# A hybrid decoder step on one core: two merges of a triangular inverse on column strips, adaLN gates by 512 columns, and 73 unread products at the start

## The chip, the cores and the metric

The kernel runs on one core of a Trainium2 chip. The metric is the device time of one execution in microseconds (us). Before the change three runs gave 2180.27, 2182.63 and 2183.85 us; the median is 2182.63 us. TensorE is called PE in the profile, its weight loads PEld, VectorE DVE, ScalarE ACT, GpSimd POOL and SyncE SP.

## The reference

One layer of a decoder trunk, for 1024 new positions of one sequence and one token each of eight others. What is computed, cut to what the change touches:

```python
mod = silu(c) @ w_ada + b_ada                   # (2048) @ (2048, 6144), 1 + 8 conditioning vectors
shift, scale, gate = split(mod, 3)
h = rmsnorm(x, norm_g) * (1 + scale) + shift
z = h @ w_in                                    # (1024 + 8, 2048) @ (2048, 8208)
...                                             # group A: gated short convolutions on half of z
# group B, per head and chunk: the gated delta rule in WY form
lmat = (k * beta) @ k.T * decay_strict
tmat = inverse(eye + lmat)                      # lower triangular
...                                             # u, o and the state by tmat, chunk after chunk
y = concatenate([y_a, o]) @ w_out               # (1024 + 8, 2048) @ (2048, 2048)
out = rmsnorm(x + gate * y, final_norm_g)
```

Everything is float32. There are 8 heads of 128 channels; the kernel takes chunks of 128 positions, four per head and half of the sequence.

## The kernel before, in words

**Layout.** Activations stand transposed: channels on the 128 partitions, positions along the free axis. The sequence is taken in two halves of 512 positions; the eight single tokens ride along with the second. The large products (`w_in`, `w_out`) split both operands into a high and a low part (`whi`/`wlo` by `split_w`, `hh`/`hl` by `make_h`, `yhi`/`ylo`) and add three products of the parts, `hh*whi`, `hl*whi` and `hh*wlo`. These are the rows `mm<-hh,whi` and so on, 512 columns wide in the first half, 256 and 264 in the second; they are most of the program.

**Stages.** First, per 128 channels, shift and scale come from `w_ada` (tiles `wat`), the normalised input `h` is made, and the first seven products with `w_in` are run beside that. Then the products of half 0 run, head by head and group by group in the hand-written table of `order`, with the delta-rule chains of the heads threaded between them. The output product of half 0 follows, then the same for half 1.

**What sets the order of the work.** The instruction order on all engines is fixed when the program is built. The class `_Order` keeps a planned time for each engine: each recorded product advances it by its `cost`, generators (`od.spawn`) wait for a planned time or for tiles (`yield`), and `pump` steps those that are due between two large products. So a changed `cost` or another number of instructions in one generator moves the positions of all later steps on every engine.

**The inverse.** For each head and half, `gdn_invert` solves the 32x32 diagonal blocks on DVE (rows `ob`, `xb`), with a round trip through memory. `gdn_apply` joins them into the 128x128 inverse `Y` of each of the four chunks. Two small merges join pairs of 32x32 blocks (`cht<-xc,dU`, then `cht<-yc,pt` and `cht<-pt,yc`). Two merges then join the halves: `pp` is the 64x64 product of `dU[0:64, c, 64:128]` and `X` (rows `cht<-X,dU`, lines 962 to 965 of the kernel), ACT writes it to `pb`, and `py` is the 64x64 product of `pb` and `Y` (rows `cht<-Y,pb`), which ACT writes to `Y`. In the order's and the trace's rows the moving operand stands behind the arrow first and the stationary one after it, as in `cht<-X,dU`. The four chunks use the same place in the array, rows 0 to 63 and columns 64 to 127 for the first of these merges, rows 64 to 127 and columns 0 to 63 for the second. After them come, per chunk, the products `cht<-st,kq`, `cht<-rt,Y`, `cht<-u,kt` and `ot<-u,dA`.

**The gates.** `gate_chunks` makes the third part of `mod` (tile `ga`, used in the output products as the factor of `y`). It runs between the large products of half 0, started 60 us of planned time after them by `conditions`, and is followed by `x1_stats`, which reads the second half of `x`. For each 128 gate columns `f`, 16 tiles of `sc` (silu of the conditioning, 32 columns of which 9 are used) are the stationary operand and blocks of `w_ada` of 128x128 the moving one; block `k` goes to column strip `k % 4` of the array, so that each strip holds a quarter of the sum. They are loaded by SP as `gw` tiles, four blocks of 128x128 to a tile, in rows of 128 numbers, and used 8 products at a time with a planned pause (`GATES`) of 7 us. After four `f` the bank is copied to `evg`, and four products with the 10-column table `selada` add the strips and transpose; four `tensor_scalar` add the bias. The tiles `gw` and `evg` share a ring of five buffers (`fx`). `raw`, the tiles of `w_in` and `w_out`, are loaded on the same SP queue, with four buffers and four more for the split parts.

**The beginning.** `norm` adds the squares of the first half of `x` on ACT, DVE and, for four of the sixteen tiles, PE (`cht<-sqt,cs`); until then PE has nothing to do. `ones` is a tile of ones that POOL writes.

PE instructions appear in the order's listing once; a float32 product counts as two records of the trace, and a transpose of one block as one.

Of the kernel before, what the change touches and what calls it, by code (L numbers as in the profile page):

```python
# [11 lines left out]
ALU = mybir.AluOpType  # L12
AX = mybir.AxisListType
# [3 lines left out]
P = 128  # L17
D = 2048
# [366 lines left out]
def _trunk(ctx, tc, nc, xT, w_in, w_ada, w_out, pack, consts, vecs, csq, ssm, yT, cap, cqp, ssp, cas, cqs, sss):  # L385
# [24 lines left out]
    def ch_tile():  # L410
        return ps_g.tile([P, 512], F32, tag="ch", name="cht", bufs=2)
# [17 lines left out]
    def pkv(n, a=0, w=None):  # L429
        o, ww = PK[n]  # L430
        return pk[:, o + a:o + a + (ww if w is None else w)]

    def ck(n, a=0, w=None):
        o, ww = CK[n]
        return cs[:, o + a:o + a + (ww if w is None else w)]
# [483 lines left out]
    def gdn_apply(half, h, hd, gp, done, cx, kq, yt):  # L919
# [41 lines left out]

        pp = ch_tile()
        for c in range(NC):
            mm(pp[64:128, c * 64:c * 64 + 64], dU[0:64, c, 64:128], X[0:64, c, 0:64], cost=0.06, start=True, stop=True,
               tile_position=(0, 64))
        pb = gp.tile([P, NC, 64], F32, tag="pb", name="pb", bufs=1)
        S.activation(pb[64:128], pp[64:128, :NC * 64].rearrange("p (c s) -> p c s", c=NC), AF.Copy, scale=-1.0)
        yield SOON
        py = ch_tile()
        for c in range(NC):  # L970
            mm(py[0:64, c * 64:c * 64 + 64], pb[64:128, c, :], Y[64:128, c, 64:128], cost=0.112, start=True, stop=True,
               tile_position=(64, 0))
        S.activation(Y[0:64, :, 64:128], py[0:64, :NC * 64].rearrange("p (c s) -> p c s", c=NC), AF.Copy)
        yield

# [402 lines left out]
            ws.add(w_out, m * P, ROWS)  # L1378


    def fx_tile(name):
        return tp.tile([P, WH], F32, tag="fx", name=name, bufs=FX)

# [19 lines left out]
    with ExitStack() as pools:  # L1403
# [38 lines left out]
        def fill(t, most=1000):  # L1442

            while most and od.now < t and queue and od.ready(hs[queue[0][0]][1], False) <= od.now:
                if next(queue[0][1], True):
                    queue.pop(0)
                most -= 1

        for _ in range(4):
            load_ada()  # L1450
        ws.ahead(0)
# [75 lines left out]
        yield  # L1527
        yield from rstd_of(acc, WH, rstd)

    GATES = 7.0  # L1530

    def gate_chunks():

        tiles = []

        def load(i):
            f, kq = divmod(i, 4)
            wt = fx_tile("gw")
            src = w_ada[kq * 512:(kq + 1) * 512, 2 * D + f * P:2 * D + (f + 1) * P]
            SY.dma_start(wt[:, :512].rearrange("p (k n) -> p k n", n=P), src.rearrange("(k p) n -> p k n", p=P))  # L1540
            tiles.append(wt)
        for i in range(4):
            load(i)
        for f in range(NK):
            if f % 4 == 0:
                ps = mm_tile()
                od.pin(ps)
            for i in (4 * f, 4 * f + 2):
                yield GATES
                yield [tiles[i][:], tiles[i + 1][:], LAND]  # L1550
                for k in range(i % 4 * 4, i % 4 * 4 + 8):
                    j = k % 4
                    mm(ps[32 * j:32 * j + 32, f % 4 * P:(f % 4 + 1) * P], sc[:, k, :],
                       tiles[f * 4 + k // 4][:, j * P:(j + 1) * P], cost=0.096 if k % 8 else 0.18,
                       start=(k < 4), stop=(k >= 12), tile_position=(0, 32 * j))
                tiles[i] = tiles[i + 1] = None
                for j in (4, 5):
                    if i + j < 4 * NK:
                        load(i + j)
            if f % 4 < 3:  # L1560
                continue
            ev = fx_tile("evg")
            S.activation(ev[:, :512], ps[:], AF.Copy)
            od.pinned.discard(ps[:].tensor.name)
            yield [ev[:, :512]]
            p2 = ch_tile()
            for i in range(4):
                mm(p2[:, i * 10:i * 10 + 10], ev[:, i * P:(i + 1) * P], ck("selada"), start=True, stop=True)
            for i in range(4):
                V.tensor_scalar(ga[:, f - 3 + i, :], p2[:, i * 10:i * 10 + 9], pkv("bada", 29 + f + i, 1), None, ALU.add)  # L1570

    conditioned = []

# [290 lines left out]
```

## Time and profile before

| what | value |
|---|---|
| median of three runs | 2182.63 us |
| the profiled execution's own time | 2179.28 us |
| its span, first to last instruction | 2177.5 us |
| PE busy, of the span | 2116.6 us (97%) |
| DVE, ACT, POOL busy | 1243.7, 829.3, 826.4 us |
| mean granted clock of PE | 0.99 |
| DMA traffic | 299.65 MB, 138 GB/s on average |

The profiled execution is 3.35 us below the median, and 1.78 us of its time lie outside the span. Times in rows of the trace are counted from the first instruction. In a row of the timeline the first number is the start, the second the length of the merged instructions, and the brackets hold the time for which the engine stood idle before it and what it waited for. Products are pipelined: the length of a row holds the drain, which overlaps with the next row, so what a product takes from the engine is the distance from its start to the start of the next. For the large products of half 0 that distance is about 0.23 us.

### The profile page before, as it was taken

The numbers are of one execution on the slowest core, as the hardware profiler recorded it, in microseconds if no ns is written. First come the engines' busy times: TensorE is split into PE (matmuls) and PEld (weight loads), VectorE is DVE, ScalarE is ACT, GpSimd is POOL, SyncE is SP. The second block draws the span as 40 slices with busy tenths as digits, with TensorE's granted clock in tenths as the row PEclk, the third lists the DMA queues.
The fourth block names the chain that finished last, engine by engine and source line by source line (L and its number), as shares of the span: only waits on it lengthen the run. The fifth ranks groups of instructions, "written<-read, shape, count | busy, mean of one in ns | idle before, by whom it ended". The sixth has DMA issues, their size and how long they took to land. (4 is left out here: it accounts for less than half of the span.)

```text
span 2177.5 us, 40451 instructions
## 1 busy us (share of the span) xinstructions
PE 2116.6 (97%) x15045; PEld 1858.7 (85%) x15045; DVE 1243.7 (57%) x3653; ACT 829.3 (38%) x1887; POOL 826.4 (38%) x801
## 2 busy tenths in 40 slices
PE   6999999999999999999999999999999999999996
PEld 3568777777778888878889999999999999999996
DVE  3436766745967636278124747657486486345544
ACT  3224333333443432353233334343343433344553
POOL 1223333433433434332434333344433343444453
PEclk8999999999999999999999999999999999999999
DMA  9984766887544456865434565557673445878777
GB/s 298 327 237 82 157 141 152 136 134 128 135 110 92 90 99 86 76 176 177 148 108 110 122 122 106 118 101 107 105 96 82 96 100 96 90 91 231 213 215 214
DMA packets 507557, 299.65 MB, mean 138 GB/s; under 512 B 37600, under 2 KB 486880, under 8 KB 507360
## 3 DMA queue, kind: packets, MB, share of 16 engines
q1 hardware_dynamic: 484656, 285.31, 61.9%
q10 hardware_dynamic: 22704, 11.77, 2.2%
q8 instruction: 118, 1.93, 0.4%
q14 instruction: 79, 0.65, 0.1%
HBM read 277.06 MB, written 19.94 MB: 136 GB/s over the span
## 5 line engine op out<-in xcount | busy, mean ns | idle before, releaser
L323 POOL TENSOR_TENSOR wlo<-raw,whi 128x512 fp32r<-128x512 f32 x529 | 709.1, 1343 | 1242.3 <-ACT whi L323 1067.9
L372 PE MATMUL mm<-hh,whi 128*128 128x264 f32 (+1 forms) x3008 | 972.5, 323 | 6.3 <-DVE y L323 2.1
L372 PE MATMUL mm<-hl,whi 128*128 128x264 f32 (+1 forms) x3008 | 971.0, 323 | 1.9 <-DVE hl L323 1.9
L372 PE MATMUL mm<-hh,wlo 128*128 128x264 f32 (+1 forms) x3008 | 971.3, 323 | 0.3 <-POOL wlo L323 0.3
L323 ACT ACTIVATE whi<-raw 128x512 fp32r<-128x512 f32 x672 | 418.8, 628 | 622.7 <-PE mm L372 377.6
L372 PEld LDWEIGHTS mm<-hh,whi 128*128 128x128 f32 x3008 | 568.5, 189 | 54.4 <-issue 8.5
L372 PEld LDWEIGHTS mm<-hl,whi 128*128 128x128 f32 x3008 | 568.8, 189 | 43.5 <-DVE hl L323 3.6
L372 PEld LDWEIGHTS mm<-hh,wlo 128*128 128x128 f32 x3008 | 568.6, 189 | 40.4 <-issue 1.0
L372 PE MATMUL mm<-yhi,wlo 128*128 128x512 f32 (+2 forms) x768 | 248.0, 323 | 6.7 <-DVE wlo L323 4.8
L372 PE MATMUL mm<-yhi,whi 128*128 128x512 f32 (+2 forms) x768 | 246.4, 321 | 0.3 <-ACT whi L323 0.2
L372 PE MATMUL mm<-ylo,whi 128*128 128x512 f32 (+2 forms) x768 | 246.2, 321 | 0.0
L323 DVE TENSOR_TENSOR ob<-tb,xb 128x62 f32<-128x62 f32 (+30 forms) x992 | 195.7, 237 | 3.9 <-DMA tb<-ub 3.9
L323 DVE TENSOR_TENSOR xb<-xb,ob 128x62 f32<-128x62 f32 (+30 forms) x992 | 193.6, 235 | 0.0
L323 DVE TENSOR_TENSOR wlo<-raw,whi 128x512 fp32r<-128x512 f32 x143 | 107.1, 754 | 98.5 <-ACT whi L323 76.4
L372 PEld LDWEIGHTS mm<-yhi,wlo 128*128 128x128 f32 x768 | 144.5, 188 | 21.7 <-DVE wlo L323 6.9
L372 PEld LDWEIGHTS mm<-ylo,whi 128*128 128x128 f32 x768 | 144.7, 188 | 12.6 <-issue 1.0
L372 PEld LDWEIGHTS mm<-yhi,whi 128*128 128x128 f32 x768 | 144.6, 188 | 12.1 <-ACT whi L323 0.9
L323 DVE SCALAR_TENSOR_TENSOR kq<-zr,pk,kq 128x512 f32<-128x512 f32 x96 | 103.5, 1078 | 3.4
L323 DVE SCALAR_TENSOR_TENSOR res<-mm,ga,xr 128x512 f32<-128x512 f32 (+2 forms) x48 | 27.3, 569 | 110.7 <-PE mm L372 101.1
L323 DVE TENSOR_TENSOR acc<-acc,sqt 128x512 f32<-128x512 f32 (+3 forms) x71 | 54.7, 773 | 26.1 <-ACT sqt L323 25.1
L323 DVE SCALAR_TENSOR_TENSOR rt<-cht,gt_neg,v 128x128 f32<-128x128 f32 x56 | 19.5, 348 | 72.0 <-PE cht L372 72.0
L323 ACT ACTIVATE u<-cht,sm 128x128 f32<-128x128 f32 x64 | 23.5, 367 | 89.1 <-DVE u L323 76.0
(403 smaller groups left out, 1979.8 us busy)
## 6 DMA issues: line engine op xcount, KB each, us to landing
raw<-in_w_in SPq DMA_DIRECT2D x488, 256.0 KB, 5.0
raw<-in_w_out SPq DMA_DIRECT2D x160, 256.0 KB, 3.4
wat<-in_w_ada SPq DMA_DIRECT2D x64, 512.0 KB, 7.3
gw<-in_w_ada SPq DMA_DIRECT2D x64, 256.0 KB, 6.2
tb<-ub ACTq DMA_DIRECT2D x16, 512.0 KB, 6.5
raw<-in_w_in SPq DMA_DIRECT2D x48, 128.0 KB, 6.0
sl<-in_ssm SPq DMA_DIRECT2D x12, 512.0 KB, 6.3
x1s<-in_xT SPq DMA_DIRECT2D x16, 260.0 KB, 5.2
```

The costliest lines, as they stand in the source:

```text
L323: r = f(*args, **kw)
L372: r = self.pe.matmul(out, lhsT, rhs, **kw)
```

## The change

Three edits, and what they move.

In the two merges each 64x64 product is cut into two of 64 rows by 32 columns on two neighbouring column strips; four products become eight, and the planned cost becomes 0.06 us for each of the eight in both merges (before 0.06 for each of four in the first and 0.112 in the second).

The gates are made 512 columns at a time: a `gw` tile is 128 rows of `w_ada` by 512 columns, four of them are loaded at a time and used by four products of 512 columns, one on each strip. 256 products of 128 columns become 64 of 512, in 16 groups with a planned pause of 14 us in place of 32 with 7. Four transposes take the place of the four products with `selada`, a `tensor_reduce` over the strips and a `tensor_tensor` with the bias that of the four `tensor_scalar`.

At the beginning, `busy(73)` writes 73 products of a 32x32 corner of `ones` with itself to a bank that nobody reads.

```diff
         pp = ch_tile()
         for c in range(NC):
-            mm(pp[64:128, c * 64:c * 64 + 64], dU[0:64, c, 64:128], X[0:64, c, 0:64], cost=0.06, start=True, stop=True,
-               tile_position=(0, 64))
+            for q in (64, 96):
+                mm(pp[q:q + 32, c * 64:c * 64 + 64], dU[0:64, c, q:q + 32], X[0:64, c, 0:64], cost=0.06,
+                   start=True, stop=True, tile_position=(0, q))
...
         py = ch_tile()
         for c in range(NC):
-            mm(py[0:64, c * 64:c * 64 + 64], pb[64:128, c, :], Y[64:128, c, 64:128], cost=0.112, start=True, stop=True,
-               tile_position=(64, 0))
+            for q in (0, 32):
+                mm(py[q:q + 32, c * 64:c * 64 + 64], pb[64:128, c, q:q + 32], Y[64:128, c, 64:128], cost=0.06,
+                   start=True, stop=True, tile_position=(64, q))
...
+    def busy(n):
+        t = ch_tile()
+        for _ in range(n):
+            mm(t[:32, :32], ones[:32, :32], ones[:32, :32], cost=0.047, start=True, stop=True)
...
+        busy(73)
         for _ in range(4):
             load_ada()
...
-    GATES = 7.0
+    GATES = 14.0
...
-        def load(i):
-            f, kq = divmod(i, 4)
-            wt = fx_tile("gw")
-            src = w_ada[kq * 512:(kq + 1) * 512, 2 * D + f * P:2 * D + (f + 1) * P]
-            SY.dma_start(wt[:, :512].rearrange("p (k n) -> p k n", n=P), src.rearrange("(k p) n -> p k n", p=P))
...
+                k, f = i % NK * P, 2 * D + i // NK * 512
+                SY.dma_start(tiles[i][:, :512], w_ada[k:k + P, f:f + 512])
...
-                for k in range(i % 4 * 4, i % 4 * 4 + 8):
-                    j = k % 4
-                    mm(ps[32 * j:32 * j + 32, f % 4 * P:(f % 4 + 1) * P], sc[:, k, :],
-                       tiles[f * 4 + k // 4][:, j * P:(j + 1) * P], cost=0.096 if k % 8 else 0.18,
-                       start=(k < 4), stop=(k >= 12), tile_position=(0, 32 * j))
...
+            for j in range(4):
+                mm(ps[32 * j:32 * j + 32, :], sc[:, k + j, :], tiles[i + j][:, :512], cost=0.23 if j else 0.41,
+                   start=(k == 0), stop=(k == 12), tile_position=(0, 32 * j))
+                tiles[i + j] = None
+            for _ in range(4):
+                load()
...
-            for i in range(4):
-                mm(p2[:, i * 10:i * 10 + 10], ev[:, i * P:(i + 1) * P], ck("selada"), start=True, stop=True)
-            for i in range(4):
-                V.tensor_scalar(ga[:, f - 3 + i, :], p2[:, i * 10:i * 10 + 9], pkv("bada", 29 + f + i, 1), None, ALU.add)
+            for j in range(4):
+                mm(p2[:, j * P:(j + 1) * P], ev[:, j * P:(j + 1) * P], ident, is_transpose=True)
+            f = i // NK * 4
+            V.tensor_reduce(ga[:, f:f + 4, :], mk(p2[:], 0, [[P, 4], [1, 9], [32, 4]]), AX.X, ALU.add)
+            V.tensor_tensor(ga[:, f:f + 4, :], ga[:, f:f + 4, :],
+                            pkv("bada", 32 + f, 4).unsqueeze(2).to_broadcast([P, 4, 9]), ALU.add)
```

What PE has in its queue at the first head's merges of half 0, before the change: a group of the gates (two `gw` tiles of four products each), and one product later the first of the two merges.

```order
L372 MATMUL mm_2693<-hh_326,wlo_2561 128x512
L372 MATMUL mm_2028<-gw_2520,sc_128 32x128 x4
L372 MATMUL mm_2028<-gw_2522,sc_128 32x128 x4
L372 MATMUL mm_2693<-hh_326,whi_2560 128x512
L372 MATMUL cht_2721<-X_2640,dU_1842 64x64 x4
L372 MATMUL mm_2693<-hl_327,whi_2560 128x512
```

The same place on PE after the change, at the second of the two merges.

```order
L372 MATMUL mm_2731<-hh_400,whi_2610 128x512
L372 MATMUL cht_2764<-Y_2676,pb_2751 32x64 x8
L372 MATMUL mm_2731<-hl_401,whi_2610 128x512
L372 MATMUL mm_2102<-gw_2597,sc_128 32x512
L372 MATMUL mm_2102<-gw_2599,sc_128 32x512
L372 MATMUL mm_2102<-gw_2601,sc_128 32x512
L372 MATMUL mm_2102<-gw_2603,sc_128 32x512
L372 MATMUL mm_2731<-hh_400,wlo_2611 128x512
```

A merge has become eight products in a row, a gate group four products of 512 columns from four tiles; the groups stand about 65 rows of the queue apart in place of about 33, and so fall at other places among the chains.

The SP queue in the gates' stage, before: two gate tiles between every two or three tiles of `w_in`.

```order
L323 DMA raw_2366<-in_w_in 128x4x128
L323 DMA raw_2402<-in_w_in 128x4x128
L323 DMA gw_2440<-in_w_ada 128x4x128
L323 DMA gw_2442<-in_w_ada 128x4x128
L323 DMA raw_2460<-in_w_in 128x4x128
L323 DMA raw_2482<-in_w_in 128x4x128
L323 DMA raw_2502<-in_w_in 128x4x128
L323 DMA gw_2520<-in_w_ada 128x4x128
L323 DMA gw_2522<-in_w_ada 128x4x128
```

And after.

```order
L323 DMA raw_2226<-in_w_in 128x4x128
L323 DMA gw_2236<-in_w_ada 128x512
L323 DMA gw_2238<-in_w_ada 128x512
L323 DMA gw_2240<-in_w_ada 128x512
L323 DMA gw_2242<-in_w_ada 128x512
L323 DMA raw_2281<-in_w_in 128x4x128
L323 DMA raw_2314<-in_w_in 128x4x128
L323 DMA raw_2356<-in_w_in 128x4x128
L323 DMA raw_2386<-in_w_in 128x4x128
L323 DMA raw_2416<-in_w_in 128x4x128
L323 DMA gw_2440<-in_w_ada 128x512
```

Four gate tiles now stand together, with four to six tiles of `w_in` between the fours. On PE the 73 products stand first in the queue, ahead of `cht<-sqt,cs`; up to the first gate group the rest of PE's queue is unchanged.

More of the change, by code (lines that the diff above doesn't have):

```diff
@@ L1528, in x1_stats, with load @@
         yield from rstd_of(acc, WH, rstd)
-    GATES = 7.0
+    GATES = 14.0
     def gate_chunks():
         tiles = []
-        def load(i):
-            f, kq = divmod(i, 4)
-            wt = fx_tile("gw")
-            src = w_ada[kq * 512:(kq + 1) * 512, 2 * D + f * P:2 * D + (f + 1) * P]
-            SY.dma_start(wt[:, :512].rearrange("p (k n) -> p k n", n=P), src.rearrange("(k p) n -> p k n", p=P))
-            tiles.append(wt)
-        for i in range(4):
-            load(i)
-        for f in range(NK):
-            if f % 4 == 0:
+        def load():
+            i = len(tiles)
+            if i < 4 * NK:
+                tiles.append(fx_tile("gw"))
+                k, f = i % NK * P, 2 * D + i // NK * 512
+                SY.dma_start(tiles[i][:, :512], w_ada[k:k + P, f:f + 512])
+        for _ in range(4):
+            load()
+        for i in range(0, 4 * NK, 4):
+            k = i % NK
+            if k == 0:
                 ps = mm_tile()
                 od.pin(ps)
-            for i in (4 * f, 4 * f + 2):
-                yield GATES
-                yield [tiles[i][:], tiles[i + 1][:], LAND]
-                for k in range(i % 4 * 4, i % 4 * 4 + 8):
-                    j = k % 4
-                    mm(ps[32 * j:32 * j + 32, f % 4 * P:(f % 4 + 1) * P], sc[:, k, :],
-                       tiles[f * 4 + k // 4][:, j * P:(j + 1) * P], cost=0.096 if k % 8 else 0.18,
-                       start=(k < 4), stop=(k >= 12), tile_position=(0, 32 * j))
[L1556 to L1560, printed above, removed]
+            yield GATES
+            yield [t[:] for t in tiles[i:i + 4]] + [LAND]
+            for j in range(4):
+                mm(ps[32 * j:32 * j + 32, :], sc[:, k + j, :], tiles[i + j][:, :512], cost=0.23 if j else 0.41,
+                   start=(k == 0), stop=(k == 12), tile_position=(0, 32 * j))
+                tiles[i + j] = None
+            for _ in range(4):
+                load()
+            if k < 12:
                 continue
@@ L1565, in gate_chunks @@
             yield [ev[:, :512]]
+            while held["ch"]:
+                yield 0.2
             p2 = ch_tile()
-            for i in range(4):
-                mm(p2[:, i * 10:i * 10 + 10], ev[:, i * P:(i + 1) * P], ck("selada"), start=True, stop=True)
-            for i in range(4):
-                V.tensor_scalar(ga[:, f - 3 + i, :], p2[:, i * 10:i * 10 + 9], pkv("bada", 29 + f + i, 1), None, ALU.add)
+            for j in range(4):
[4 more added lines that the diff above has]
+                            pkv("bada", 32 + f, 4).unsqueeze(2).to_broadcast([P, 4, 9]), ALU.add)
     conditioned = []
```

## The prediction

> **What bounds the kernel.** I read the page first, then the busy time by stretches, then the waits of PE. The page's line of busy times:
>
> ```profile
> PE 2116.6 (97%) x15045; PEld 1858.7 (85%) x15045; DVE 1243.7 (57%) x3653; ACT 829.3 (38%) x1887; POOL 826.4 (38%) x801
> ```
>
> PE is the only engine near its span. That is an average, so the stretches come next: the beginning, and all that follows it (PE, PEld, DVE, ACT, POOL busy, then the granted clock, the DMA share and GB/s).
>
> ```profile
> 18.50:35.50 17.00, 11.96 (x103) 8.92 (x104) 6.46 (x9) 3.76 (x7) 5.23 (x4) 0.50 1.08 265
> 56.00:59.40 3.40, 2.91 (x28) 1.33 (x32) 2.81 (x6) 3.08 (x5) 1.19 (x1) 0.51 1.10 348
> 59.40:2177.00 2117.60, 2079.59 (x14757) 1837.69 (x14749) 1222.40 (x3615) 808.90 (x1853) 818.93 (x788) 0.99 0.64 133
> ```
>
> From 59.4 us on PE is busy for 2079.6 of 2117.6 us: 38.0 us are left for all waits together. So a microsecond taken from PE's queue there comes off the end, unless it turns into a wait. Before that, the DMA share is 1.08 and 1.10 and the clock is at half for 17 us: another regime. The waits of PE from 60 us on show what could take a gain back: many kinds, each of a few us, the longest single one 2.1 us.
>
> ```profile
> PE mm L372 <- DVE wlo L323: 4.8, 6, 1.6
> PE cht L372 <- DVE acc L323: 3.7, 2, 2.1
> ...
> PE cht L372 <- ACT pb L323: 1.6, 1, 1.6
> ```
>
> The sum is therefore made of what each group of small products takes from PE, start to start.
>
> **The gates.** A group of the gates in the timeline of PE, between large products:
>
> ```profile
> 310.10 0.40 PE L372 MATMUL mm<-hl,whi 128*128 128x512 f32 x1
> 310.43 0.64 PE L372 MATMUL mm<-gw,sc 128*32 128x128 f32 x16
> 311.00 0.50 PE L372 MATMUL mm<-hh,wlo 128*128 128x512 f32 x1
> 311.34 0.40 PE L372 MATMUL mm<-hh,whi 128*128 128x512 f32 x1
> ```
>
> From 310.10 to 311.34 are 1.24 us, of which two large products would take 2 x 0.23; the group costs 0.78 us. It is 0.57 of its own (310.43 to 311.00) and about 0.21 for going over to strips and back. There are 512 records in all, 16 to a group, so 32 groups, 25.0 us:
>
> ```profile
> L372 PE MATMUL mm<-gw,sc 128*32 128x128 f32 x512 | 20.7, 279 | 0.0
> ```
>
> No product of 512 columns on four strips is in this trace, but the first stage has the same shape at 256 columns, in groups of four and of eight products (8 and 16 records):
>
> ```profile
> 88.52 1.07 PE L372 MATMUL tpt<-wat,sc 128*32 128x256 f32 x16
> 89.52 0.50 PE L372 MATMUL cht<-hh,whi 128*128 128x512 f32 x1
> ...
> 90.42 0.64 PE L372 MATMUL tpt<-wat,sc 128*32 128x256 f32 x8
> 90.99 0.50 PE L372 MATMUL ot<-hh,whi 128*128 128x512 f32 x1
> ```
>
> The four of 256 columns take 0.57 us, exactly as the eight of 128: it is columns that cost, not instructions. The eight of 256 take 1.00, so 1024 more columns cost 0.43 and 0.14 is fixed. Four products of 512 columns have the columns of the latter: 1.00, with the same 0.21 around them 1.21 us. Sixteen groups are 19.4 us in place of 25.0: **5.6 us less**. The saving is that of sixteen fixed parts of 0.35 us. If a 512-column stream ran no better than separate groups (1.56 for two), it would be nothing; if the fixed part vanished altogether (16 x 0.86 = 13.8) it would be 11.2. I take 5.6, since the rows at 256 columns are the same instruction at half the length.
>
> The four `selada` products against a group of four transposes of 128x128 blocks:
>
> ```profile
> 521.66 0.95 PE L372 MATMUL cht<-cs,evg 128*128 128x10 f32 x8
> 522.47 0.48 PE L372 MATMUL mm<-hl,whi 128*128 128x512 f32 x1
> ```
>
> ```profile
> 212.99 0.60 PE L372 MATMUL tpt<-cs,v 128*128 128x128 f32 x4
> 213.34 0.48 PE L372 MATMUL mm<-hh,wlo 128*128 128x512 f32 x1
> ```
>
> 0.81 becomes 0.35, four times: **1.8 us less**. What DVE does with them (one reduction and one addition over 36 columns in place of four small operations) lies beside PE; the bank they read has a second one behind it, and `ga` is read only by the output products. I cost it at nothing. If PE waited for it each time, the whole of a 512-column operation on DVE is an upper bound, 0.75 us four times, 3.0 us:
>
> ```profile
> L323 DVE TENSOR_TENSOR wlo<-raw,whi 128x512 fp32r<-128x512 f32 x143 | 107.1, 754 | 98.5 <-ACT whi L323 76.4
> ```
>
> The loads: SP issues the same 64 transfers of 256 KB, four in a row in place of two, and the tiles of `w_in` stand behind them. PE has the split parts of several tiles in hand, so this is cover as long as these are there. Where it is thinnest, from 400 to 520 us, the transfers take (KB each, us to landing):
>
> ```profile
> raw<-in_w_in SPq DMA_DIRECT2D x34, 256.0 KB, 7.1
> gw<-in_w_ada SPq DMA_DIRECT2D x24, 256.0 KB, 7.6
> ```
>
> I cost it at nothing and keep the other case as a rival.
>
> **The merges.** One of them, and the nearest group of products on two places of the array at once:
>
> ```profile
> 291.72 0.68 PE L372 MATMUL cht<-X,dU 64*64 64x64 f32 x8
> 292.32 0.50 PE L372 MATMUL mm<-hl,whi 128*128 128x512 f32 x1
> ```
>
> ```profile
> 287.25 0.44 PE L372 MATMUL cht<-xc,dU 32*32 32x32 f32 x16
> 287.62 0.50 PE L372 MATMUL mm<-hh,wlo 128*128 128x512 f32 x1
> ```
>
> A merge takes 0.60 us: 0.14 fixed, as above, and 0.46 for eight records one after another, 0.058 each. After the change there are eight records on each of two strips, each still 64 columns. In the `wat` rows the eight further records are two of 256 columns on each of four strips and cost 0.43, that is 0.84 ns per column of a strip, so eight of 64 take 0.43, and with the fixed part 0.57 if the strips run side by side. That is 0.03 less. Both kinds have 128 records in all, eight to a merge, so 32 merges:
>
> ```profile
> L372 PE MATMUL cht<-Y,pb 64*64 64x64 f32 x128 | 10.8, 224 | 1.6 <-ACT pb L323 1.6
> L372 PE MATMUL cht<-X,dU 64*64 64x64 f32 x128 | 10.8, 225 | 0.0
> ```
>
> **1.0 us less.** Cutting a product by its stationary columns does not shorten the stream that each strip must see. The bounds: the `xc` group, 16 records in 0.37, would give 7.4 us less, but its stream is 32 columns and the merges' is 64; strips that take turns would need 16 x 0.058 + 0.14 = 1.06 a merge, 14.7 us more. I take 0.57, which follows the rows with strips.
>
> The rows that speak for side by side are the gates': 16 records of 128 columns in 0.57 us on strips that share all 128 rows, whose weight loads lie inside that time:
>
> ```profile
> 240.89 0.45 PEld L372 LDWEIGHTS mm<-gw,sc 128*32 128x32 f32 x16 [0.36 <-issue]
> ```
>
> The Trainium skill, page "TensorE: Matmul & The Clock Gate", Part 3, says that a weight load overlaps with products in flight only where its row group differs; the two strips of a merge share their rows, so by that rule they would take turns and the sum would be 7.3 us worse than no change in place of 8.4 better. The trace disagrees for the gates' strips, and no merge on strips is in it.
>
> **The 73 products.** Until its first product PE only waits, and what the 73 need, `ones`, POOL has written by 0.93 us; below it stand PE's first row and two later waits that end with a transfer:
>
> ```profile
> 0.73 0.20 POOL L323 MEMSET ones<- 128x128 f32 x1 [0.29 <-POOLq L1841]
> ```
>
> ```profile
> 8.47 3.71 PE L372 MATMUL cht<-sqt,cs 128*128 128x512 f32 x4 [8.47 <-ACT sqt L323]
> ...
> 51.54 0.64 PE L372 MATMUL tpt<-wat,sc 128*32 128x256 f32 x8 [0.92 <-DMA wat<-in_w_ada]
> 53.05 0.64 PE L372 MATMUL tpt<-wat,sc 128*32 128x256 f32 x8 [0.87 <-DMA wat<-in_w_ada]
> ```
>
> The `xc` group has eight products on two places, 0.23 us beyond the fixed part, so 0.058 for one product on one place; 73 take 4.2 us at full clock and 8.4 at half, and end between 5 and 9.4 us. At worst the first `sqt` product starts 0.9 us late, with a faster clock to make it up. What could be won is PE time before 53 us, and there PE stands waiting for `wat` to land: any lead ends in a longer wait. The half clock from 18.5 to 35.5 us begins 9 us or more after the last of the 73. So **nothing**; bounds 2 us either way. The same page, Part 1, has the clock fall back after an idle window of about 3.4 us; the trace agrees in kind, with 0.50 in the row from 18.50.
>
> **Sum.** 5.6 + 1.8 + 1.0 = 8.4 us. The profiled execution of 2179.28 would take 2170.9; it lies 3.35 below the median, so the median of 2182.63 becomes **2174.2 us**. About 0.2%, 4.4 us, is what a measurement of this kernel can tell from no change: faster is below 2178.3, slower above 2187.0.
>
> **Rivals.** *New waits eat it.* The order is re-planned, and almost every row behind the first gate group stands elsewhere among the chains. A misplaced step costs up to 2.1 us of wait, and a pause can bring a half-clock window after it, as at 56 us (3.4 us at 0.51: 1.7 lost). Two such, 2 x 3.8 = 7.6, give 2181.8, no change. For: the waits of 38.0 us are of just this kind. Against: as many can vanish as appear. Chance 0.20.
>
> *More than the sum.* The gates' tiles come in rows of 512 numbers in place of 128, the crowded stretch eases, and the wait for `pb` (1.6, with 1.7 of half clock behind it) goes; if also 1.8 of the half clock in the beginning reached the end: 8.4 + 3.3 + 1.8 = 13.5, 2169.1 us. Against: the wait for `pb` is one among many. Chance 0.15.
>
> *The strips of a merge take turns.* 14.7 more in the merges against 7.4 less in the gates: 2189.9 us, slower. It decides once a merge takes 0.23 us more than before (0.83 in place of 0.60). Against: the gates' strips. Chance 0.07.
>
> *Four loads in a row starve the products.* Two more transfers ahead of `w_in` are 0.52 MB, 3.6 us at the 147 GB/s of 400 to 520 us; for the six fours there up to 21.6 us if nothing covered it, and 2185 if half did. For: ACT waits there 22.1 us for `raw` to land. Against: PE doesn't.
>
> ```profile
> DMA packets 34525, 17.70 MB, mean 147 GB/s; under 512 B 2179, under 2 KB 34120, under 8 KB 34514
> ...
> ACT whi L323 <- DMA raw<-in_w_in: 22.1, 11, 4.5
> ```
>
> Chance 0.05.
>
> **How the numbers follow.** My forecast has 0.53, the rivals 0.20, 0.15, 0.07 and 0.05. The likeliest alone reaches from 2169 to 2179. The range takes in the larger gain below and the eaten one above: 2167 to 2184 us; the two slower cases and the far ends of the others, under 0.2, are left out. Faster: 0.50 of the forecast, 0.15, and 0.03 of the eaten case, 0.68. Slower: 0.07, 0.04, and 0.02 of the eaten one, 0.13. Within: 0.19.
>
> **What would show it.** In the changed profile: 16 gate groups of about 1.00 us to the next product, transposes of 0.35, merges near 0.57, and PE's idle time after 60 us still near 38 us. Merges above 0.8 would make the strips' rival right; idle time above 44 us the re-planning one; waits for `whi` or `wlo` between 400 and 520 us the loads'. The forecast is wrong if a gate group takes more than 1.5 us, or if the time to 60 us moves by more than 2 us.

## The result, and the profile after

The changed kernel takes **2163.91 us** (median of 4 runs, 2161.51 to 2165.11) beside 2183.06 of the kernel before (4 runs): ratio 0.9913, 95% interval 0.9896 to 0.9930. That is 19.1 us less, where 8.4 were forecast and 13.5 was the far case. The profiled executions differ by 17.8 (2161.51 against 2179.28); the rows in this section are from these two.

The three priced terms came out as worked out. PE's timeline of the changed kernel shows one place of each kind: a gate group, one merge of each sort, the transposes.

```profile
278.00 1.07 PE L372 MATMUL mm<-gw,sc 128*32 128x512 f32 x8
279.00 0.50 PE L372 MATMUL mm<-hh,wlo 128*128 128x512 f32 x1
...
292.04 0.64 PE L372 MATMUL cht<-X,dU 64*32 64x64 f32 x16
292.61 0.50 PE L372 MATMUL mm<-hl,whi 128*128 128x512 f32 x1
...
294.19 0.64 PE L372 MATMUL cht<-Y,pb 64*32 64x64 f32 x16
294.76 0.49 PE L372 MATMUL mm<-hl,whi 128*128 128x512 f32 x1
...
297.20 0.60 PE L372 MATMUL cht<-cs,evg 128*128 128x128 f32 x4
297.56 0.48 PE L372 MATMUL mm<-hh,wlo 128*128 128x512 f32 x1
```

Start to start: 1.00 us for a gate group (forecast 1.00), 0.57 for each merge (0.57), 0.36 for the transposes (0.35). So 8.4 us are in the work, and some ten more are elsewhere. Two rows of PE's busy time by stretches show where; first before, then after, each from 64 us to the last whole microsecond before the last product that both have (the transposition of `rsm`):

```profile
64.00:2167.00 2103.00, 2075.06 (x14730) 1835.72 (x14722) 1214.83 (x3599) 808.52 (x1852) 813.96 (x781) 1.00 0.63 132
```

```profile
64.00:2148.00 2084.00, 2062.12 (x14599) 1818.30 (x14598) 1217.20 (x3585) 807.07 (x1852) 823.11 (x790) 1.00 0.64 133
```

PE's idle time (length less busy) falls from 27.9 to 21.9 us. The rest is clock: before had four windows of 3.40 us at half clock in this stretch, 1.7 us lost in each, and after has none. PE is busy all through such a window, so its busy time counts the lost time as work. These are the four, before, and the same stretches after, where the granted clock (third number from the end) is 1.00:

```profile
445.10:448.50 3.40, 3.40 (x12) 2.92 (x12) 0.98 (x5) 0.37 (x1) 1.38 (x2) 0.51 0.83 126
649.90:653.30 3.40, 3.40 (x12) 2.70 (x11) 3.40 (x17) 0.79 (x2) 2.53 (x3) 0.51 0.83 171
1465.70:1469.10 3.40, 3.40 (x18) 3.40 (x18) 2.28 (x3) 1.57 (x4) 1.18 (x1) 0.51 0.16 37
1506.70:1510.10 3.40, 3.40 (x18) 3.40 (x17) 3.40 (x22) 0.63 (x1) 1.27 (x1) 0.51 0.29 87
```

```profile
445.10:448.50 3.40, 3.40 (x23) 2.12 (x22) 0.70 (x2) 0.78 (x3) 0.00 (x0) 1.00 0.94 139
...
1506.70:1510.10 3.40, 3.40 (x30) 3.40 (x30) 2.58 (x11) 1.14 (x2) 0.47 (x1) 1.00 1.00 55
```

The first of them stands behind the wait for `pb` that the prediction quoted: PE's timeline of before has it at 443.38, and the window begins 1.7 us later.

```profile
441.17 0.64 PE L372 MATMUL mm<-gw,sc 128*32 128x128 f32 x16
443.38 0.68 PE L372 MATMUL cht<-Y,pb 64*64 64x64 f32 x8 [1.57 <-ACT pb L323]
```

The beginning is slower in this profile, not faster: PE's 100th large product starts at 86.8 us in place of 84.6, 2.2 later. The 73 products end at 8.98 us, inside the forecast's 5 to 9.4, and little of their delay is left soon after: the `wat` products that started at 36.15 us start at 36.29. Then a `wat` tile lands later, for which PE waits 2.23 us where the prediction's row of 51.54 had 0.92, and the half clock from 55.8 us lasts 6.8 us in place of 3.4. PE's first row and that wait, then the stretch, after:

```profile
0.99 7.99 PE L372 MATMUL cht<-ones 32*32 32x32 f32 x146 [0.99 <-POOL nhalf L323]
...
52.99 0.64 PE L372 MATMUL tpt<-wat,sc 128*32 128x256 f32 x8 [2.23 <-DMA wat<-in_w_ada]
```

```profile
55.80:62.60 6.80, 5.76 (x41) 3.67 (x42) 4.11 (x8) 3.10 (x6) 2.16 (x2) 0.51 1.10 349
```

The books, by the start of the transposition of `rsm`, the last product of both kernels: 2167.03 before (first row) and 2148.38 after (second), 18.7 less.

```profile
2167.03 0.43 PE L372 MATMUL cht<-cs,rsm 128*128 128x128 f32 x2 [1.02 <-POOL rsm L323]
```

```profile
2148.38 0.69 PE L372 MATMUL cht<-cs,rsm 128*128 128x128 f32 x2 [1.03 <-POOL rsm L323]
```

Work 8.4, idle time 6.0, four windows 6.8, together 21.2, less 2.2 at the beginning: 19.0, with 0.3 that no row explains. So waits and the half clock behind them brought 12.8 us, more than the work.

Whether a wait has a half-clock window behind it is in part luck. PE's timeline has the same wait in both kernels, before (first row) with the last of the four windows 1.2 us behind it, and after (second row) with none:

```profile
1505.55 0.38 PE L372 MATMUL mm<-hh,whi 128*128 128x256 f32 x1 [2.06 <-DVE y L323]
```

```profile
1490.07 0.39 PE L372 MATMUL mm<-hh,whi 128*128 128x256 f32 x1 [2.06 <-DVE y L323]
```

Over all executions the mean granted clock is 0.9883 before (62 executions, 0.985 to 0.992) and 0.9905 after (4, 0.989 to 0.992). That is some 5 us of 2170, so most of the 6.8 us isn't luck. All this says where the time went; the experiments ask why.

### The profile page after: what moved, and what is told of

Its sections match the earlier page's. It is cut to its first block, busy times and chain, and to the rows that moved or that the text cites. A ratio compares the mean times of both kernels' runs of the same rounds, so it can differ in the third digit from the quotient of the medians.

```text
span 2159.7 us, 40441 instructions
## 1 busy us (share of the span) xinstructions
PE 2111.2 (98%) x15047; PEld 1849.6 (86%) x15047; DVE 1244.5 (58%) x3636; ACT 827.9 (38%) x1887; POOL 835.9 (39%) x810
## 3 DMA queue, kind: packets, MB, share of 16 engines
q1 hardware_dynamic: 460080, 285.31, 62.1%
## 4 chain that ended last, share of the span: by engine, by line
PE 85%; DMA 6%; DVE 4%; ACT 2%; issue 1%; POOL 1%; SPq 1%; ACTq 0%; DVEq 0%; POOLq 0%
PE mm L372 74%; PE cht L372 5%; PE tpt L372 4%; DMA raw<-in_w_out 2%; DMA raw<-in_w_in 1%; PE ot L372 1%; DMA x1s<-in_xT 1%; POOL wlo L323 1%; DMA wat<-in_w_ada 1%; DVE ob L323 1%; SPq L323 1%; DVE wlo L323 1%; ACT whi L323 1%; DMA x<-in_xT 1%; DVE xb L323 0%
## 5 line engine op out<-in xcount | busy, mean ns | idle before, releaser
L323 POOL TENSOR_TENSOR wlo<-raw,whi 128x512 fp32r<-128x512 f32 x538 | 719.6, 1340 | 1215.0 <-ACT whi L323 1045.4
L323 DVE TENSOR_TENSOR ob<-tb,xb 128x62 f32<-128x62 f32 (+30 forms) x992 | 204.5, 246 | 1.1 <-DMA tb<-ub 1.1
L323 DVE TENSOR_TENSOR xb<-xb,ob 128x62 f32<-128x62 f32 (+30 forms) x992 | 182.6, 224 | 0.0
L372 PEld LDWEIGHTS mm<-ylo,whi 128*128 128x128 f32 x768 | 144.6, 188 | 13.3 <-issue 1.0
L323 DVE TENSOR_TENSOR acc<-acc,sqt 128x512 f32<-128x512 f32 (+3 forms) x71 | 49.9, 705 | 24.6 <-ACT sqt L323 23.7
```

What stands on the lines that cost most here:

```text
L323: r = f(*args, **kw)
L372: r = self.pe.matmul(out, lhsT, rhs, **kw)
```

## The experiments

Theory one, from this comparison: the new order behind the gates removes waits. The rival: one of the three parts does something that the forecast had not priced. In what follows the *mark* is the start of the transposition of `rsm` in the profile of each run; what is added behind it runs too late to delay it.

**The parts alone.** Three kernels with one part each, and one that has the instructions of before but plans both merges at the costs of the changed ones:

```
 gates_alone       before + gates on strips, transposes, GATES 14
 merges_alone      before + merges on column strips
 busy_alone        before + busy(73)
 merge_costs_only  before, and
-  mm(pp[64:128, ...], dU..., X..., cost=0.06
+  mm(pp[64:128, ...], dU..., X..., cost=0.12
-  mm(py[0:64, ...], pb..., Y..., cost=0.112
+  mm(py[0:64, ...], pb..., Y..., cost=0.12
```

Expected of the gates: 

> The kernel before with the gates' edit alone (512 columns on four strips, transposes, loads in rows of 512 numbers, pause of 14). The changed kernel measured 19.1 us below the one before, 10.7 more than the sum of PE work (8.4). The sum: 7.4 us less, about 2175.7 us. The gates theory (all of the rest comes with the gates' form and its loads): 16 to 19 us less, about 2165. The order theory (each re-planned order has its own waits and its own half-clock windows behind them): anywhere from 2 to 14 us less, with PE's idle time and the number of half-clock windows after 60 us moving by as much as the time departs from 7.4.

Of the merges: 

> The kernel before with the merges' edit alone. The sum: a merge takes 0.57 us to the next product in place of 0.60, 1.0 us less, about 2182.0 us. The gates theory: the same. The order theory: within 6 us of that on either side, and near the kernel with the planned costs alone, since its order is the same.

Of the products: 

> The kernel before with the 73 unread products alone. The sum: no difference, 2183 us, within 2 us. A theory that the warm clock of the start is worth something: 2 us less or more, and a different length of the half clock between 18 and 62 us. The order theory: the planned time of all that follows is shifted alike, so the order of the products stays nearly the same and so does the time.

Of the costs: 

> The kernel before with the two merges' planned cost alone changed to what the changed kernel plans for them (0.48 us a merge, as 4 x 0.12): the same instructions, in another order. The sum: no difference, 2183 us, within 1 us. The gates theory: no difference. The order theory: a difference of 2 to 6 us either way, seen as other waits on PE and another number of half-clock windows, with the same PE work.

Measured against 2183.66 us: gates 2237.80 (ratio 1.0249, interval 1.0234 to 1.0265), merges 2180.11 (0.9982, 0.9973 to 0.9991), products 2182.28 (0.9991, 0.9982 to 0.9999), costs alone 2178.46 (0.9976, 0.9967 to 0.9986). The part that was to bring 7.4 us *lost 54*. The sum of the parts is +49, the whole is -19. The merges on strips show no gain over their planned costs without strips. In gates_alone, ACT waits for weights to land; these waits over the whole span (sum, times, longest), and the large queue's row of the page (packets, MB, share of the 16 engines' time):

```profile
ACT whi L323 <- DMA raw<-in_w_in: 217.7, 81, 5.9
```

```profile
q1 hardware_dynamic: 460080, 285.31, 71.6%
```

The same two of before:

```profile
ACT whi L323 <- DMA raw<-in_w_in: 81.4, 36, 4.8
```

```profile
q1 hardware_dynamic: 484656, 285.31, 61.9%
```

It moves the same 285.31 MB in fewer packets, and yet the packets take 71.6% of the engines' time in place of 61.9%. Already between 100 and 200 us, where both programs issue the same in the same order, the mean of the 512-byte packets in the trace is 38 ns against 33. The first gate tile is issued only at 236.7 us, so it isn't the four loads in a row that are slow; packets are slow ahead of them too.

**The parts in pairs**, and the gates again:

```
 gates_again    = gates_alone
 gates_busy     gates_alone  + busy(73)
 gates_merges   after        - busy(73)
 merges_busy    merges_alone + busy(73)
```

> The kernel with the gates' edit alone once more, unchanged. It measured 2237.8 us, 54 us above the one before; its PE waits after 60 us were 71.6 us in place of 28.4, and its 512-byte packets took longer already between 100 and 200 us (38.1 ns on average, the others 32.8 to 33.8), where its order is still the same as that of all the others. The order theory (the re-planned order alone makes the waits): the same again, 2235 to 2243. A placement theory (where this program's tensors lie in memory makes its transfers slow, and that changes from one loading to the next): another time, 2175 to 2185, with packets of 33 ns.

> The gates' edit and the 73 products, without the merges' edit. On every engine its order is that of the gates alone but for the 73 products. The order theory: 2235 to 2243 us, as the gates alone. A placement theory that hangs on the program: any time, from 2165 to 2240, and packets of 33 or 38 ns between 100 and 200 us according to it. The sum: 2175.7.

> The changed kernel without the 73 products; on every engine its order is the changed kernel's but for them. The order theory: the changed kernel's time, 2164 us, within 3 us. The sum: 2175. A placement theory: any time from 2160 to 2240. A theory that the 73 products make the changed kernel fast: 2175 us or more.

> The changed kernel without the gates' edit; its order is that of the merges alone but for the 73 products. The merges alone measured 2180.1 us and the 73 products alone 1.4 us less than nothing. The order theory and the sum: 2178 to 2181 us. A placement theory: any time.

Measured against 2183.93: 2240.57 (1.0256, 1.0240 to 1.0272), so the loss repeats; 2208.28 (1.0112, 1.0097 to 1.0127); 2167.73 (0.9928, 0.9911 to 0.9944); 2205.40 (1.0101, 1.0085 to 1.0117). The 73 products leave the order of all other instructions as it is, on every engine. Yet they bring 30 us to the gates alone, cost 25 with the merges alone, bring 4 with both (whose intervals with and without them overlap), and nearly nothing to before. So the order alone doesn't set the time. Either their time at the beginning matters, or their being in the program.

**Products that shift nothing.** The 73 behind everything else; 1 MB of unused DRAM; other numbers of them at the beginning:

```
 gates_busy_end  gates_alone, at the very end:  + busy(73)
 gates_spare     gates_alone, ahead of the DRAM scratch: + spare = dp.tile([P, 2048], F32)
                 at the very end: + SY.dma_start(spare[:, :P], ones)
 after_n40       after, - busy(73) + busy(40)
 after_n146      after, - busy(73) + busy(146)
```

> The gates alone took 2237.8 and 2240.6 us, and 2208.3 with the 73 unread products at the beginning, though each engine's instructions stand in the same order in both. Here the 73 products stand behind everything else, where they shift nothing in time ahead of them and cost at most about 4.3 us at the end (73 x 0.058). Theory one (phase): what the products at the beginning change is the time at which the work meets its transfers; then the gates alone stay as they were: 2238 to 2245 us. Theory two (placement): what they change is the length of the program and with it where instructions, lists of transfers and buffers lie in memory; then the time moves by over 10 us here too, towards 2212 or elsewhere, and the 512-byte packets between 100 and 200 us, 38 ns on average in the gates alone and 33 in the other kernels, change with it.

> The gates alone, and 1 MB of unused DRAM taken ahead of the kernel's other scratch buffers (one 64 KB store to it at the very end, 2 to 3 us). Phase: nothing moves before the end, so 2238 to 2245 us. Placement of the scratch buffers: the time moves by over 10 us. If neither this nor the products at the end moves it, but the products at the beginning did, phase is left.

> The changed kernel with 40 unread products in place of 73. The order of all other instructions is the same as with 73 (2163.9 us) and with none (2167.7). Theory one, that the products' number acts through the phase or the placement: another time, anywhere within some tens of us of these, up or down. The rival, that the changed order is robust and only the other two orders are fragile: 2162 to 2169 us.

> The changed kernel with 146 unread products, 8.5 us at full clock and up to 17 at half, so that they reach past 8.5 us, where the first real product stood, by some us. If the start is all: 2164 plus 0 to 8 us. If the changed order is robust, 2162 to 2172. If the phase decides, a time that may differ from 2164 by tens of us.

Measured against 2180.96: 2203.64 (1.0105, 1.0089 to 1.0120), 2232.87 (1.0241, 1.0226 to 1.0257), 2169.48 (0.9947, 0.9931 to 0.9964), 2156.65 (0.9891, 0.9876 to 0.9906). The products at the end bring as much as at the beginning, though every real instruction stands ahead of them: the phase (the time at which the work meets its transfers) is out. So is the scratch memory, as far as 1 MB moves it: 1.0241 beside 1.0249 and 1.0256. What counts is that the program is longer. after_n146 has the lowest time of all; its interval and that of the changed kernel overlap, so it isn't shown to be faster than that one.

Laid out by the number of TensorE's records, the shares line up, whatever the order of the instructions; the marks do so only among kernels of one order (share: the large queue's row of the page):

| records of PE | runs | share, % | mark, us |
|---|---|---|---|
| 14645 | gates_alone, again, spare | 71.6, 71.6, 71.2 | 2230.6, 2223.9, 2220.8 |
| 14791 | gates_busy, gates_busy_end | 68.8, 68.2 | 2196.0, 2191.9 |
| 14901 | gates_merges | 65.8 | 2152.2 |
| 14981 | after_n40 | 65.2 | 2156.6 |
| 15045 | before, merge_costs_only | 61.9, 62.5 | 2167.0, 2168.8 |
| 15047 | after | 62.1 | 2148.4 |
| 15191, 15193 | busy_alone, after_n146 | 60.0, 59.0 | 2168.0, 2146.8 |
| 15301 | merges_alone | 58.7 | 2165.2 |
| 15447 | merges_busy | 58.1 | 2193.0 |

The gates take 400 records out of the program, the merges put 256 in, the 73 products 146: with all three the program is as long as before, to two records.

**Is it the length, and whose?** Four more, of which two bring the gates to the length of before:

```
 gates_end200        gates_alone, at the very end: + busy(200)
 gates_dve_end       gates_alone, at the very end:
                     + for _ in range(292): V.memset(ones[:32, :1], 1.0)
 gates_costs_end200  gates_end200, both merges planned at cost=0.12 (not on strips)
 merges_end73        merges_alone, at the very end: + busy(73)
```

> The gates alone with 200 unread products (400 records) behind everything else, so that TensorE's program has 15045 records, as many as before. Length theory: the large queue's share falls to that of the other programs of this length, 61.5 to 63%, as measured up to the end of the real work, and the time, without the products at the end (up to 11.6 us), falls from 2238 to 2170 to 2195. Rival (the 73 products happened to hit a good placement; the relation is chance): a share anywhere from 58 to 72%.

> The gates alone with 292 one-column MEMSETs on VectorE behind everything else: as many instructions as the 146 records (each a weight load and a product) of the 73 products. If any instruction's place in memory counts: share about 68.5% instead of 71.6 and, without the MEMSETs' own time at the end (some 20 us), about 2205 us. If only TensorE's program counts: 71 to 72% and 2235 to 2242 us without them.

> The gates on four strips, the merges' products as before but planned at the changed merges' costs (so that every engine's order is that of the changed kernel, the merges' products apart), and 200 unread products at the end, so that the program has 15045 records. If the new order is what the changed kernel gains beyond the sum: 2164 plus 1.0 for the merges' work, plus up to 11.6 at the end: 2165 to 2178 us, and 10 us or more under gates_end200. If the strips of the merges matter by themselves: over 2178. If the order is nothing once the length is equal: the same as gates_end200.

> The merges alone with the 73 products at the end. Merges alone took 2180, with the products at the beginning 2205, with packets as quick (58.7 and 58.1% of the large queue). If that loss is of the length too (15447 records being more than what helps): 2203 to 2210 us. If it came from the beginning, where PE reached its first wait for a transfer 1.4 us earlier: 2180 to 2186.

Measured against 2179.88: 2188.82 (1.0040, 1.0026 to 1.0054), 2261.26 (1.0371, 1.0350 to 1.0392), 2171.95 (0.9960, 0.9947 to 0.9973), 2198.10 (1.0083, 1.0068 to 1.0098). With as many records as before the gates alone are as quick with their transfers as before; the queue's row and ACT's waits in gates_end200:

```profile
q1 hardware_dynamic: 460080, 285.31, 61.2%
```

```profile
ACT whi L323 <- DMA raw<-in_w_in: 60.1, 26, 4.3
```

The mark moves from 2230.6 to 2162.2 us by instructions that run behind it. 292 instructions more on VectorE, as many as the 73 products' weight loads and products together, do nothing of the kind: the mark is 2223.0. The share is 70.0% of a span that is longer by the MEMSETs; share times span is 1583 us, beside 1589 to 1605 in gates_alone, gates_again and gates_spare, and 1503 in gates_busy_end. So it is TensorE's program; of the other engines only VectorE was tried.

At equal length the parts can be priced. The marks of gates_end200 and of gates_costs_end200, in PE's timeline:

```profile
2162.23 0.43 PE L372 MATMUL cht<-cs,rsm 128*128 128x128 f32 x2 [1.03 <-POOL rsm L323]
```

```profile
2147.46 0.69 PE L372 MATMUL cht<-cs,rsm 128*128 128x128 f32 x2 [1.03 <-POOL rsm L323]
```

From 2167.0 (before) the gates bring 4.8 us and the order that follows from the merges' *planned costs* 14.8; the changed kernel, which has the strips and the 73 products besides, has its mark 0.9 later (2148.4). The marks hold the beginning, which differs between profiles: the 100th large product starts at 84.6, 86.3, 84.8 and 86.8 us in these four. Counted from there, the gates bring 6.4, the order 13.3 and the strips 1.1. Each is read from one profile, and two profiles of one kernel (gates_alone and gates_again) have marks 6.7 us apart, so only the order's part is clear of that. The medians give the same picture: less what the 200 products add behind the mark (11.6 and 13.0 us in the two profiles, by span less mark against before's 10.5) they are 2177.2 and 2159.0 beside 2179.88, that is 2.7 for the gates and 18.2 for the order. With the old gates the same change of plan brought 5.2 (merge_costs_only).

gates_end200 and gates_costs_end200 have the same instructions. Counted in large products, the second falls 12.2 us ahead between the 1500th (505 us in both) and the 1800th (587 against 599), of which 2.6 go again by the 2100th. PE's timeline and clock there in gates_end200:

```profile
568.16 0.71 PE L372 MATMUL cht<-st,kq 128*128 128x128 f32 x4 [0.67 <-DVE st L323]
571.78 0.80 PE L372 MATMUL cht<-rt,Y 128*128 128x128 f32 x2 [2.90 <-DVE rt L323]
577.51 0.77 PE L372 MATMUL cht<-u,kt 128*128 128x128 f32 x2 [4.94 <-DVE ob L323]
578.07 0.63 PE L372 MATMUL ot<-u,dA 128*128 128x128 f32 x2
```

```profile
570.00:583.70 13.70, 6.99 (x21) 5.73 (x22) 10.30 (x65) 6.10 (x20) 1.28 (x1) 0.51 0.32 106
```

In PE's queue the steps of a chain stand one behind another with no large product between them, so each wait is open (0.67, 2.90, 4.94: 8.5 us). 13.7 us at half clock go with it, in which PE is busy for 7.0, so about 3.5 more are lost. The longest wait has a second cause. In DVE's queue an addition of `x1_stats` (`acc<-acc,sqt`) stands ahead of the chain's `u`; it waits for ACT's `sqt`, and that for a tile `x1s` to land. ACT and DVE there:

```profile
575.73 0.64 ACT L323 ACTIVATE sqt<-x1s 128x520 f32<-128x520 f32 x1 [3.61 <-DMA x1s<-in_xT]
```

```profile
576.40 0.70 DVE L323 TENSOR_TENSOR acc<-acc,sqt 128x520 f32<-128x520 f32 x1 [3.40 <-ACT sqt L323]
577.02 0.34 DVE L323 TENSOR_SCALAR u<-cht,sm 128x128 f32<-128x128 f32 x1
```

In gates_costs_end200 the same steps have large products between them:

```profile
562.60 0.39 PE L372 MATMUL mm<-hl,whi 128*128 128x512 f32 x1
562.83 0.38 PE L372 MATMUL cht<-rt,Y 128*128 128x128 f32 x2
562.97 0.48 PE L372 MATMUL mm<-hh,wlo 128*128 128x512 f32 x1
...
566.05 0.46 PE L372 MATMUL cht<-u,kt 128*128 128x128 f32 x2
566.27 0.48 PE L372 MATMUL mm<-hh,wlo 128*128 128x512 f32 x1
566.59 0.38 PE L372 MATMUL ot<-u,dA 128*128 128x128 f32 x2
```

```profile
550.00:590.00 40.00, 38.56 (x181) 30.97 (x180) 38.12 (x136) 19.68 (x54) 17.55 (x17) 1.00 0.54 125
```

merges_end73 keeps most of the loss of merges_busy (its mark is 19.6 us behind the 2165.2 without the products, that of merges_busy 27.8), so that too is mostly of the length: beyond some 15300 records more of them cost time.

**A draw, and a limit.** Another order at equal work and length, and more length with the changed order:

```
 after_gates12  after
-    GATES = 14.0
+    GATES = 12.0
 after_end200   after, at the very end: + busy(200)
```

> The changed kernel with the gates' pause in the plan at 12 in place of 14: the same instructions and the same length (15047 records), the gates' groups come sooner and the order behind them is another. If the order is a draw: a time anywhere from 2155 to 2185 us, with the difference to 2164 in PE's waits and the half-clock windows behind them, and the large queue's share still 61 to 63%. If the changed work itself removes the waits: within 4 us of 2164.

> The changed kernel with 200 more unread products at the end, so 15447 records, as many as the merges alone with the 73. Merges alone lost 18 to 25 us there against 15301 records. If that loss belongs to the length: the last real product moves from 2148.4 to 2160 us or more. If it belongs to the merges' order: 2145 to 2151, and up to 21 us behind it for the products (as measured in gates_end200).

Measured against 2182.35: 2175.31 (0.9966, 0.9954 to 0.9978) and 2212.28 (1.0132, 1.0114 to 1.0151). after_gates12 has the same instructions, the same length and the same share (62.4%), and its mark is at 2161.6, 13.2 later than in the changed kernel. 7.9 us are lost between the 300th and the 1200th large product, and 12.3 between the 1500th and the 1800th, with the clock at half from 577.9 to 584.7; 6.3 of these come back by the 2100th. Here too the steps of a chain stand in a row, from 576.85 to 581.85 us, with waits of 1.79, 2.09 and 0.84 us and no such wait of DVE for `sqt` among them. So the changed order is one draw among others, and a good one. after_end200 has its mark at 2188.2, 40 us behind the changed kernel with the same order. Its packets are quick (57.5%), but the transfers are not; landing and ACT's waits there:

```profile
raw<-in_w_in SPq DMA_DIRECT2D x488, 256.0 KB, 5.8
```

```profile
ACT whi L323 <- DMA raw<-in_w_in: 135.5, 57, 5.6
```

After has 5.1 us and 59.4 (24 times). So the length acts from both sides: as far as tried, least is lost between 15045 and 15301 records. How much it costs hangs on the order: the changed one has marks of 2152.2 and 2156.6 with 14901 and 14981 records, while the gates' own loses tens of us with 14645 and 14791. Why the length acts stays open. Shown is that it isn't the phase (the products at the end), the scratch memory as far as it was moved (gates_spare) or VectorE's program (gates_dve_end). The load of fetching instructions is unlikely to be it: the queues for that move 2.5 to 2.6 MB in each run, in 0.4 to 0.5% of the engines' time. That where instructions, lists of transfers or data lie in memory moves with the length of the program is argued, not shown: no run could place them.

## Why the prediction was wrong, point by point

*The sum.* Right in its three terms to 0.01 us for each group shown. At equal length, counted from the 100th large product, the gates brought 6.4 of 7.4 and the strips 1.1 of 1.0, as near as single profiles can tell. The gates' part was by turns more and less: gates_end200 is 9.1 us ahead of before at the 1500th large product and, behind the stall at 570 us, 1.4 behind it at the 1800th.

*"The 73 products: nothing."* The reasons held: PE only waits there, and before alone hardly moves (0.9991). The price held too. The same products behind everything else in gates_end200, first at full clock and then at half:

```profile
2162.60:2163.70 1.10, 1.10 (x36) 1.10 (x36) 0.58 (x2) 0.38 (x1) 0.54 (x1) 1.00 0.00 0
2164.00:2183.00 19.00, 19.00 (x361) 19.00 (x359) 2.85 (x9) 0.00 (x0) 2.63 (x4) 0.50 0.35 113
```

That is about 0.06 us for a product of two records at full clock (forecast 0.058) and 0.105 at half; the 0.109 of the beginning (7.99 / 73) is near the price at half clock. (The profile of after has no record of the clock before 14.7 us, and its views give 1.00 there.) Nor do the runs show that they cost the 2.2 us of the beginning: kernels without them there, with the same order up to that place, have their 100th large product anywhere from 83.9 us (merges_end73) to 89.2 (gates_again), and those with them from 84.6 (merges_busy) to 88.1 (gates_busy). What "nothing" left out is what no view of before shows: they set the length of PE's program, worth 30 us with the gates alone and at most a few with both other parts.

*"So a microsecond taken from PE's queue there comes off the end, unless it turns into a wait."* This step failed, together with the sizes of the rivals that hang on it. The sum puts the change of waits and clock at nothing, since as many waits can vanish as appear, and the rivals let it be 7.6 us one way or 5.1 the other. It was 12.8: 6.0 of waits and 6.8 of half clock, and the time fell 3 us below the range. Two things were missed. The row from 59.4 us on counts half clock as busy, so the 38.0 us are not all that a new order can change. And waits are a draw by the order: at one place 12 us lie between two orders of the same instructions, because a chain without large products between its steps, and a late transfer behind one of them, open three waits, with half the clock for 13.7 us. The rival "new waits eat it" had this mechanism with the sign turned and at 0.6 of the size. "More than the sum" named the wait for `pb` and the half-clock window behind it, and that one did go (1.6 and 1.7), but it counted one window where four went, and a gain at the beginning that didn't come. How far a draw can go is shown by after_gates12: with the same work and the same length it is 11 us above the changed kernel by the medians. The forecast had no way to tell a good order from a bad one, so that this change got a good one is luck.

*"The strips of a merge take turns."* Ruled out: 16 records on two strips take 0.57 us, where 1.06 was the price of taking turns. The Trainium skill's rule, page "TensorE: Matmul & The Clock Gate", Part 3, that a weight load overlaps with products in flight only where its row group differs, doesn't hold here: the strips share their rows, and the trace has all sixteen weight loads of the first merge within 0.48 us.

*"Four loads in a row starve the products."* Seen in gates_alone (217.7 us of waits for `raw`), but the loads aren't the cause: gates_end200 issues the same loads in the same order and waits 60.1.

*The checks.* PE's idle time from 59.4 us on went from 38.0 to 32.6 (the row below), not "near 38". The time to 60 us moved by more than 2 us, by the prediction's own words a sign that it was wrong, though a weak one: the beginning differs by as much between kernels that share it.

```profile
59.40:2159.20 2099.80, 2067.24 (x14633) 1820.73 (x14625) 1225.46 (x3600) 809.45 (x1857) 829.59 (x797) 1.00 0.64 134
```

## What to carry to other kernels

Where a planner lays out the order, price the work first, then ask how far two plans of the same work lie apart: here 13 us, half as much again as the work that was saved. It is cheap to try: change one planned cost and look for stretches in which PE's steps of one chain stand next to each other, and for an instruction that waits for a transfer ahead of such a step in another engine's queue. Test the parts of a change at an equal number of instructions on TensorE, or a part's loss may be the program's length. A busy time holds the lost clock, so read it together with the granted clock.

## What the runs showed of the hardware

- The large queue's packets took 71.6% of the DMA engines' time with 14645 records in TensorE's program and 57.5% with 15447, for the same bytes; the time was least between. The 400 records that bring gates_alone to the length of before run after everything else and moved the mark by 59 to 68 us.
- PE lost half its clock for 3.4 us after a wait of 1.57 us (before, 443.38) and after one of 2.06 (before, 1505.55), and kept it after another of 2.06 (after, 1490.07). Before's stretch of 3.4 us ahead of the first window:

```profile
441.70:445.10 3.40, 1.83 (x21) 1.57 (x16) 0.00 (x0) 2.99 (x6) 1.30 (x2) 1.00 0.93 173
```

  The Trainium skill, "TensorE: Matmul & The Clock Gate", Part 1, has the clock fall after an idle window of about 3.4 us; here the window ahead of 445.1 was more than half busy (1.83 of its 3.4 us).
- Sixteen fp32 records of 64 columns, with 32 stationary columns each, take 0.57 us on two column strips that share their rows; eight with 64 stationary columns each take 0.60 on one place. The strips run side by side, but a product cut by its stationary columns gains next to nothing.
